# Attention in batches of four key tiles, with row-tiled scores, maxima in turn and split GpSimd additions

## The chip, the cores and the metric

The kernel runs on one core of one Trainium2 chip. The metric is the time of one execution in microseconds of the device (us). Engines are named as in the profile: PE (TensorE's matmuls), PEld (its weight loads), DVE (VectorE), ACT (ScalarE), POOL (GpSimd), and SP (SyncE, whose queue, SPq, issues the DMAs).

## The reference

Two layers work on a sequence of 2048 tokens of width 1024. Each layer projects the normalized input to attention heads, a short convolution and a 2-D Fourier mixer, multiplies each with a gate, joins them and projects back. The change touches the attention: 8 query heads of width 64, which share 2 key/value heads. In float32 it is

```python
scores = jnp.einsum('bqkgd,bskd->bkgqs', qb, k) * HEAD_DIM ** -0.5
p = jax.nn.softmax(scores, axis=-1)
o = jnp.einsum('bkgqs,bskd->bqkgd', p, v)        # every query sees all 2048 keys
y_attn = o * jax.nn.silu(g_a)
```

## The kernel before

A layer runs the input projection (`in_proj`), then the attention with the Fourier mixer as background work (`attention`), then the output projection (`out_proj`). The attention has 16 units in a layer: 4 chunks of 512 queries by 4 pairs of heads. A unit handles its two heads together, against 16 key tiles of 128 keys.

Scores are computed with the keys on the partitions: a tile of probabilities is 128 keys by 512 queries for each of two heads. So that the exp can't overflow, the maximum of each query's scores over all keys is found beforehand by a cheaper product with the queries on the partitions (`row_max`): for one of 4 query tiles and one of 4 key chunks, two matmuls of 64 rows, one per head (the head on partitions 0 to 63 and the one on 64 to 127), then a DVE maximum each. 16 such pairs make a unit. When the last is done, the negated maxima are transposed (`guard_row`) and written by two small DMAs over a row of the unit's second query tile, where they act as one more term of the product. They run ahead of the scores: `LEAD` is 6 pairs beyond one unit.

Products keep float32's accuracy by splitting operands into a rounded part (hi) and a rest (lo). The key tile `kk1` holds the hi part twice (rows 0 to 63 and 64 to 127); the query tile of a head, `qq1`, holds its hi part on 64 rows and its lo part on the others, so that one matmul over 128 rows gives two terms. A second matmul pairs `kk2` (a row of ones, then the keys' lo part) with `qq2` (the guard row, then the queries' hi part). `scores` issues these two (lines 854, 855) for each head of a key tile, and ACT takes the exp out of PSUM (line 856) into a probability tile, one of 8 buffers (4 `XA`, 4 `WL`).

`weigh` multiplies the tile with the values (line 866; the two heads write two halves of the partitions of one PSUM bank, so they run on two halves of the array's columns) and adds it to a running sum for the softmax denominator (lines 874, 876): on DVE for the key tiles in `DVE_KT`, on GpSimd for the others. In the last unit of a layer DVE adds all. `sums` turns the running sums into row sums, `finish` multiplies the result by the gate, the reciprocal of the sums and splits it into hi and lo, in steps spread over the batches of the next unit.

`attention` writes the order of PE, ACT, DVE and GpSimd out by hand. It goes through a unit in 6 batches of 3, 3, 2, 3, 3 and 2 key tiles. A batch issues a step of background work (`background`: the Fourier mixer, 28 steps in a layer, 16 of them with matmuls, later the first output weights), the scores of its key tiles, as many pairs of `row_max`, and the weighing of the batch before:

```python
            for kt in tiles:
                self.scores(u, kt)
            self.max_pairs(pairs)
            ...
                for kt in self.BATCHES[c]:
                    self.weigh(self.units[v], kt)
```

PSUM has 8 banks: 7 with the tag `A` (scores, maxima, transposes, sums, Fourier), one with the tag `C` (the weighed sum).

The projections are products over 128 rows; the last part of `in_proj` runs the first maxima (`first_unit`) between its matmuls.

Of the kernel before, what the change touches and what calls it, by code (L numbers as in the profile page):

```python
# [13 lines left out]
P = 128  # L14
D = 1024
S = 2048
# [22 lines left out]
class Trunk:  # L39
# [34 lines left out]
    def setup(self):  # L74
# [10 lines left out]
        self.zero = self.const("zero", [P, 4])  # L85
        nc.gpsimd.memset(self.zero, 0.0)
# [316 lines left out]
    def do_q(self, l, grp, tabs):  # L403
# [5 lines left out]
        def q_trans(ch, sl, qn):  # L409
# [167 lines left out]
    def fourier_mix_mats(self, l):  # L577
# [3 lines left out]
        for b in range(2):  # L581
            fm = self.small("fm", [P, HD], bufs=2)
# [177 lines left out]
    LEAD = 6  # L760
    BATCHES = ((0, 1, 2), (3, 4, 5), (6, 7), (8, 9, 10), (11, 12, 13), (14, 15))
    NBT = len(BATCHES)

    def q_load(self, u):

        src = self.q1[u["ch"]][u["pr"] // 2][:, u["pr"] % 2]
        u["qq1"] = [self.t("TAB", [P, CH], F32R) for _ in range(2)]
        for h in range(2):
            self.nc.sync.dma_start(u["qq1"][h].bitcast(F32), src[:, h, :])
        u["qq2"], u["mx"] = [], [self.small("mx", [P, 4, 4]) for _ in range(2)]  # L770
        u["nm"] = self.small("nm", [P, 2, 4], F32R, bufs=3)

    def q_copy(self, u, h):

        src = self.q1[u["ch"]][u["pr"] // 2][:, u["pr"] % 2, h, :]
        q2 = self.t("QS", [P, CH], F32R)
        for r in ([slice(0, P)] if h else [slice(0, HD), slice(HD, P)]):
            dr = r if h else slice(HD - r.start, P - r.start)
            self.nc.sync.dma_start(q2.bitcast(F32)[dr], src[r])
        u["qq2"].append(q2)  # L780

    def row_max(self, u, i):

        nc = self.nc
        s, kc = i // 4, i % 4
        pss = [self.p("A") for _ in range(2)]
        for h in range(2):
            r = slice(h * HD, (h + 1) * HD)
            nc.tensor.matmul(pss[h], u["qq1"][h][r, s * P:(s + 1) * P], self.kk1[u["kv"]][kc][r], start=True, stop=True)  # L789

        def reduce():
            for h in range(2):
                nc.vector.tensor_reduce(out=u["mx"][h][:, s, kc:kc + 1], in_=pss[h], axis=AX.X, op=ALU.max)  # L793
            if i == 15:
                for h in range(2):
                    nc.vector.tensor_reduce(out=u["nm"][:, h, :], in_=u["mx"][h], axis=AX.X, op=ALU.max, negate=True)
                self.gq.append(u)
        return reduce

    def guard_row(self, u):  # L800
# [6 lines left out]
        for h in range(2):  # L807
            nc.sync.dma_start(u["qq2"][h].bitcast(F32)[0:1, :], nt.bitcast(F32)[4 * h:4 * h + 4, :])

    def max_before(self, i):  # L810

        for ui, u in enumerate(self.units):
# [3 lines left out]
            elif o in (8, 10):  # L816
                self.q_copy(u, o // 2 - 4)

    def max_pairs(self, pairs):

        while self.gq:
            self.guard_row(self.gq.pop(0))
        todo = [self.row_max(self.units[j // 16], j % 16) for j in pairs if 0 <= j < 16 * len(self.units)]
        for reduce in todo:
            reduce()
# [17 lines left out]
    DVE_KT = (0, 3, 8, 11), range(NKT)  # L843

    def scores(self, u, kt):
# [5 lines left out]
        ks = slice((kt % 4) * P, (kt % 4 + 1) * P)  # L851
        for h in range(2):
            ps = self.p("A")
            nc.tensor.matmul(ps, self.kk1[kv][kt // 4][:, ks], u["qq1"][h], start=True, stop=False)  # L854
            nc.tensor.matmul(ps, self.kk2[kv][kt // 4][:, ks], u["qq2"][h], start=False, stop=True)  # L855
            nc.scalar.activation(pt[:, h, :], ps, AF.Exp, scale=HD ** -0.5)  # L856

    def weigh(self, u, kt):
# [8 lines left out]
        w = "d" if kt in self.DVE_KT[u is self.units[-1]] else "p"  # L867
        eng = nc.vector if w == "d" else nc.gpsimd
        acc, pend = u["acc"], u["pend"]
        if acc[w] is None:  # L870
            pend[w].append(pt)
            if len(pend[w]) == 2:
                acc[w] = self.t("WH", [P, 2, CH])
                eng.tensor_tensor(acc[w], pend[w][0], pend[w][1], ALU.add)  # L874
        else:
            eng.tensor_tensor(acc[w], acc[w], pt, ALU.add)  # L876
# [17 lines left out]
    def finish(self, u, k):  # L894
# [5 lines left out]
        elif k == 3:  # L900
# [4 lines left out]
            for h in range(2):  # L905
                nc.sync.dma_start(u["sm"][h * HD:(h + 1) * HD, :], d[h * CH:(h + 1) * CH].partition_broadcast(HD))
        elif k == 4:
            nc.vector.tensor_tensor(u["y"], u["y"], u["sm"], ALU.mult)
        elif k == 5:
# [5 lines left out]
    def attention(self, l):  # L915
        self.yat = {}
        n = len(self.units)
        for g in range((n + 1) * self.NBT):
            ui, b = divmod(g, self.NBT)
            u = self.units[ui] if ui < n else None  # L920
            tiles = self.BATCHES[b]
# [244 lines left out]
```

## Time and profile before

| | |
|---|---|
| time, median of 3 runs | 2721.76 us (2720.47 to 2722.68) |
| the profiled execution: its time, its span | 2718.48 us, 2716.6 us |
| PE busy | 2664.5 us, 98% of the span |
| DVE busy | 1821.2 us, 67% |
| GpSimd busy | 1032.7 us, 38% |
| ACT busy | 891.0 us, 33% |
| mean DMA rate | 102 GB/s |
| maxima, line 793, DVE | 632.9 us in 1024 instructions |
| weighing, line 866, PE | 271.3 and 267.8 us for the two kinds of tile |

The span runs from the first to the last instruction; the time is the execution's own. Busy time of PE says that matmuls were in flight, not that it ran at its peak. The attention of the two layers lies at about 575 to 1193 us and 1906 to 2525 us.

### The profile page before, as it was taken

To read this page: it belongs to the slowest core of one execution; us is meant where nothing else is said; L and a number is where in the kernel's file an instruction comes from. 1 tells how busy PE (TensorE), PEld (TensorE's weight loads), DVE (VectorE), ACT (ScalarE), POOL (GpSimd) and SP (SyncE) were. 2 spreads that over 40 slices of the span, in tenths; PEclk is the share of its full clock that TensorE was granted. 3 is DMA by queue.
4 is the path that set the end of the run, shared out by engine and by line. 5 is a ranking of instruction groups with operands and counts; after the bars stand their busy time and mean duration, and the time that the engine had idled before them with its cause. 6 is when DMAs were issued, how large, how long until landed. Compare 5 with 4: busy or idle time off the path is not lost.

```text
span 2716.6 us, 36918 instructions
## 1 busy us (share of the span) xinstructions
PE 2664.5 (98%) x13748; PEld 1867.2 (69%) x13748; DVE 1821.2 (67%) x3072; ACT 891.0 (33%) x1789; POOL 1032.7 (38%) x597
## 2 busy tenths in 40 slices
PE   7999999999999999999999999999999999999998
PEld 5987898765555555557898889887565555554686
DVE  6655673457788788786785347534678888778655
ACT  3321421133444444430232124211444444444200
POOL 0200020035786777703331001100558777774134
PEclk9999999999999999999999999999999999999999
DMA  9754362333221111144446123522323111111332
GB/s 302 225 138 149 108 189 72 98 101 121 80 58 44 48 48 48 36 129 156 147 132 186 55 94 98 151 79 85 111 74 105 48 48 47 45 31 51 121 132 93
DMA packets 192516, 277.34 MB, mean 102 GB/s; under 512 B 40400, under 2 KB 103248, under 8 KB 191824
## 3 DMA queue, kind: packets, MB, share of 16 engines
q1 hardware_dynamic: 192336, 274.98, 33.1%
q8 instruction: 108, 1.77, 0.3%
q14 instruction: 72, 0.59, 0.1%
HBM read 213.68 MB, written 69.48 MB: 104 GB/s over the span
## 4 chain that ended last, share of the span: by engine, by line
PE 91%; DVE 4%; DMA 2%; issue 1%; POOL 1%; ACT 1%; SPq 0%; POOLq 0%; DVEq 0%; ACTq 0%
PE psC L866 16%; PE psA L854 9%; PE psA L329 8%; PE psA L330 8%; PE psA L331 8%; PE psA L855 8%; PE psA L789 6%; PE psA L1028 4%; PE psA L1026 4%; PE psA L1027 4%; PE psA L302 3%; PE psA L304 3%; PE psA L303 3%; PE psA L885 1%; PE psA L706 1%
## 5 line engine op out<-in xcount | busy, mean ns | idle before, releaser
L793 DVE TENSOR_REDUCE mx<-psA 128x1 f32<-128x512 f32 x1024 | 632.9, 684 | 238.5 <-PE psA L789 236.3
L876 POOL TENSOR_TENSOR WH<-WH,XA 128x1024 f32<-128x1024 f32 x150 | 362.5, 2417 | 211.1 <-ACT XA L856 208.4
L854 PE MATMUL psA<-TAB,KK 128*128 128x512 f32 x1024 | 421.8, 412 | 0.0
L855 PE MATMUL psA<-QS,KK 128*128 128x512 f32 x1024 | 403.3, 394 | 0.0
L329 PE MATMUL psA<-H,WH 128*128 128x512 f32 x1008 | 397.9, 395 | 0.0
L330 PE MATMUL psA<-H,WH 128*128 128x512 f32 x1008 | 393.4, 390 | 0.0
L331 PE MATMUL psA<-H,WL 128*128 128x512 f32 x1008 | 393.0, 390 | 0.0
L876 POOL TENSOR_TENSOR WH<-WH,WL 128x1024 f32<-128x1024 f32 x150 | 361.4, 2409 | 63.2 <-ACT WL L856 53.8
L856 ACT ACTIVATE XA<-psA 128x512 f32<-128x512 f32 x512 | 281.0, 611 | 307.0 <-PE psA L855 226.3
L856 ACT ACTIVATE WL<-psA 128x512 f32<-128x512 f32 x512 | 281.6, 615 | 161.2 <-PE psA L855 161.0
L854 PEld LDWEIGHTS psA<-TAB,KK 128*128 128x128 f32 x1024 | 192.3, 188 | 155.2 <-issue 87.2
L866 PE MATMUL psC<-XA,V 128*64 128x512 f32 x1024 | 271.3, 608 | 5.8 <-DVE EV L899 5.8
L866 PE MATMUL psC<-WL,V 128*64 128x512 f32 x1024 | 267.8, 601 | 0.0
L128 DVE TENSOR_TENSOR WL<-WR,WH 128x512 fp32r<-128x512 f32 (+2 forms) x272 | 126.0, 500 | 210.0 <-ACT WH L125 204.5
L874 POOL TENSOR_TENSOR WH<-WL,XA 128x1024 f32<-128x1024 f32 x30 | 71.0, 2366 | 446.1 <-DVE mx L793 378.4
L329 PEld LDWEIGHTS psA<-H,WH 128*128 128x128 f32 x1008 | 189.6, 188 | 46.3 <-issue 7.4
L302 PE MATMUL psA<-WH,H 128*128 128x256 f32 x768 | 219.8, 287 | 0.0
L125 ACT ACTIVATE WH<-WR 128x512 fp32r<-128x512 f32 (+2 forms) x280 | 119.4, 479 | 305.3 <-PE psA L330 112.1
L855 PEld LDWEIGHTS psA<-QS,KK 128*128 128x128 f32 x1024 | 192.2, 188 | 37.7
L304 PE MATMUL psA<-WH,H 128*128 128x256 f32 x768 | 216.4, 284 | 0.6 <-DVE H L128 0.6
L303 PE MATMUL psA<-WL,H 128*128 128x256 f32 x768 | 216.8, 283 | 0.0
L331 PEld LDWEIGHTS psA<-H,WL 128*128 128x128 f32 x1008 | 189.3, 188 | 39.8
(215 smaller groups left out, 4010.5 us busy)
## 6 DMA issues: line engine op xcount, KB each, us to landing
WR<-in_w_in SPq DMA_DIRECT2D x176, 256.0 KB
WR<-in_w_ada SPq DMA_DIRECT2D x64, 256.0 KB
q<-EV SPq DMA_DIRECT2D x128, 128.0 KB
TAB<-q SPq DMA_DIRECT2D x64, 256.0 KB
H<-dft SPq DMA_DIRECT2D x64, 256.0 KB
XA<-in_x SPq DMA_DIRECT2D x24, 512.0 KB
XA<-x SPq DMA_DIRECT2D x20, 512.0 KB
dft<-in_k_dft SPq DMA_DIRECT2D x32, 256.0 KB
```

Of the source, the lines that this page charges most:

```text
L302: nc.tensor.matmul(ps[:, s2, :], hh[b][:, sl], w1, start=(b == 0), stop=False)
L303: nc.tensor.matmul(ps[:, s2, :], hh[b][:, sl], w2, start=False, stop=False)
L304: nc.tensor.matmul(ps[:, s2, :], hl[b][:, sl], w1, start=False, stop=(b == NB - 1))
L329: nc.tensor.matmul(ps, w1, hh[b], start=(b == 0), stop=False)
L330: nc.tensor.matmul(ps, w1, hl[b], start=False, stop=False)
L331: nc.tensor.matmul(ps, w2, hh[b], start=False, stop=(b == NB - 1))
L793: nc.vector.tensor_reduce(out=u["mx"][h][:, s, kc:kc + 1], in_=pss[h], axis=AX.X, op=ALU.max)
L854: nc.tensor.matmul(ps, self.kk1[kv][kt // 4][:, ks], u["qq1"][h], start=True, stop=False)
L855: nc.tensor.matmul(ps, self.kk2[kv][kt // 4][:, ks], u["qq2"][h], start=False, stop=True)
L856: nc.scalar.activation(pt[:, h, :], ps, AF.Exp, scale=HD ** -0.5)
L866: nc.tensor.matmul(u["pv"][h * HD:(h + 1) * HD, :], v, pt[:, h, :], start=(kt == 0), stop=(kt == NKT - 1))
L876: eng.tensor_tensor(acc[w], acc[w], pt, ALU.add)
```

## The change

- Scores are row-tiled: query tiles now hold both heads (head 0 on rows 0 to 63, head 1 on 64 to 127), one tile for hi and one for lo, and a key tile's scores are four terms, each a pair of 64-row matmuls for the two heads into two PSUM banks. The fourth term takes the guard row: a constant `sel` with ones in rows 0 and 64 picks rows 0 and 64 of a tile `g`, which is loaded with queries first (`guard_load`), and whose two rows the guard's DMAs overwrite.
- A unit is 4 batches of 4 key tiles. In a batch scores (S) and maxima (M) are issued in the order SSMSMSMM, and each pair's DVE maxima right behind its matmuls. `LEAD` is 8.
- The guard transpose is issued at the beginning of the second batch after the last maxima, ahead of background work and scores (`guard_rows`).
- GpSimd's addition of a probability tile is two instructions, one per head, issued in `scores`; DVE's stays one and in `weigh`. DVE takes key tiles 3, 7, 11 and 15.
- The steps of `finish` are spread over 4 batches and the first of the unit after.
- The queries' and keys' layouts follow: `q_trans` stores hi and lo with two DMAs, `do_kv` puts the keys' rest on both halves. The buffer `fm` of `fourier_mix_mats` has one copy.

```diff
+        sel = self.t("HS", [P, P])
+        nc.gpsimd.memset(sel, 0.0)
+        for h in range(2):
+            nc.gpsimd.memset(sel[h * HD:h * HD + 1, :], 1.0)
+        self.sel = self.const("sel", [P, P], F32R)
+        nc.vector.tensor_copy(self.sel, sel)
...
-            for h in range(2):
-                r, o = slice(h * HD, (h + 1) * HD), slice((1 - h) * HD, (2 - h) * HD)
-                nc.sync.dma_start(self.q1[ch][grp][r, :, h, sl], hi.bitcast(F32)[r])
-                nc.sync.dma_start(self.q1[ch][grp][o, :, h, sl], lo.bitcast(F32)[r])
+            for j, t in enumerate((hi, lo)):
+                nc.sync.dma_start(self.q1[ch][grp][:, :, j, sl], t.bitcast(F32))
...
-            nc.vector.tensor_tensor(kl[:, :, :, HD:], k4, khf[:, :, :, 0:HD], ALU.subtract)
-            kl3 = kl.rearrange("p a b d -> p (a b) d")
-            nc.vector.tensor_copy(kl3[:, :, 0:1], self.ones[:, 0:4].unsqueeze(2))
-            nc.vector.tensor_copy(kl3[:, :, 1:HD], self.zero.unsqueeze(2).to_broadcast([P, 4, HD - 1]))
+            for j in range(2):
+                nc.vector.tensor_tensor(kl[:, :, :, j * HD:(j + 1) * HD], k4, khf[:, :, :, 0:HD], ALU.subtract)
...
-            fm = self.small("fm", [P, HD], bufs=2)
+            fm = self.small("fm", [P, HD], bufs=1)
...
-    LEAD = 6
-    BATCHES = ((0, 1, 2), (3, 4, 5), (6, 7), (8, 9, 10), (11, 12, 13), (14, 15))
-    NBT = len(BATCHES)
+    LEAD = 8
+    ORDER = "SSMSMSMM"
+    BATCH = len(ORDER) // 2
+    NBT = NKT // BATCH
...
+        u["q"] = [self.t("TAB", [P, CH], F32R) for _ in range(2)]
+        for j in range(2):
+            self.nc.sync.dma_start(u["q"][j].bitcast(F32), src[:, j, :])
...
-    def q_copy(self, u, h):
...
+    def guard_load(self, u):
+
+        u["g"] = self.t("QS", [P, CH], F32R)
+        self.nc.sync.dma_start(u["g"].bitcast(F32), self.q1[u["ch"]][u["pr"] // 2][:, u["pr"] % 2, 0, :])
...
-            self.gq.append(u)
+            self.gq.append([u, 2])
...
+    def guard_rows(self):
+
+        for e in list(self.gq):
+            e[1] -= 1
+            if not e[1]:
+                self.guard_row(e[0])
+                self.gq.remove(e)
...
-    DVE_KT = (0, 3, 8, 11), range(NKT)
+    DVE_KT = (3, 7, 11, 15), range(NKT)
...
+        k1, k2, (q1, q2) = self.kk1[kv][kt // 4][:, ks], self.kk2[kv][kt // 4][:, ks], u["q"]
+        pss = [self.p("A") for _ in range(2)]
+        terms = (k1, q1), (k1, q2), (k2, q1), (self.sel, u["g"])
+        for i, (k, q) in enumerate(terms):
+            for h in range(2):
+                r = slice(h * HD, (h + 1) * HD)
+                nc.tensor.matmul(pss[h], k[r], q[r], start=i == 0, stop=i == len(terms) - 1)
         for h in range(2):
-            ps = self.p("A")
-            nc.tensor.matmul(ps, self.kk1[kv][kt // 4][:, ks], u["qq1"][h], start=True, stop=False)
-            nc.tensor.matmul(ps, self.kk2[kv][kt // 4][:, ks], u["qq2"][h], start=False, stop=True)
-            nc.scalar.activation(pt[:, h, :], ps, AF.Exp, scale=HD ** -0.5)
+            nc.scalar.activation(pt[:, h, :], pss[h], AF.Exp, scale=HD ** -0.5)
+        self.add(u, kt, pt, "p")
...
+        if w == "d":
+            self.nc.vector.tensor_tensor(acc[w], a, pt, ALU.add)
         else:
-            eng.tensor_tensor(acc[w], acc[w], pt, ALU.add)
+            for h in range(2):
+                self.nc.gpsimd.tensor_tensor(acc[w][:, h], a[:, h], pt[:, h], ALU.add)
...
+        for g in range((n + 2) * self.NBT):
...
+            if 0 < ui <= n and b == 2:
+                self.sums(self.units[ui - 1])
+            self.guard_rows()
...
+            self.background()
+            at = {"S": 0, "M": 0}
+            for c in self.ORDER:
+                if c == "M":
+                    self.max_pairs((pair + at[c],))
+                elif u:
+                    self.scores(u, first + at[c])
+                at[c] += 1
             if 0 < g <= n * self.NBT:
                 v, c = divmod(g - 1, self.NBT)
+                for j in range(self.BATCH):
+                    self.weigh(self.units[v], self.BATCH * c + j)
...
+            for back in (1, 2):
+                if 0 <= ui - back < n:
+                    self.finish(self.units[ui - back], b + self.NBT * (back - 1))
```

## Rows read from the trace of the kernel before

**Rows 1.** The page's first part: busy time, share of the span, instructions.

```profile
PE 2664.5 (98%) x13748; PEld 1867.2 (69%) x13748; DVE 1821.2 (67%) x3072; ACT 891.0 (33%) x1789; POOL 1032.7 (38%) x597
```

**Rows 2.** Chain of waits from 900 to 980 us: start, length, what.

```profile
904.54 2.74 PE psC L866 x12
...
917.70 1.87 PE psC L866 x8
...
941.65 2.73 PE psC L866 x12
```

**Rows 3.** Windows, one unit: length, busy of each engine, clock, DMA share, GB/s.

```profile
904.54:941.65 37.11, 37.11 (x180) 19.16 (x181) 29.82 (x43) 17.21 (x34) 26.36 (x12) 1.00 0.17 44
```

**Rows 4.** PE in order of time: start, length, line, matmuls merged.

```profile
903.57 0.98 PE L789 MATMUL psA<-KK,TAB 64*128 64x512 f32 x6
...
909.97 0.40 PE L855 MATMUL psA<-QS,KK 128*128 128x512 f32 x1
910.30 0.74 PE L789 MATMUL psA<-KK,TAB 64*128 64x512 f32 x4
910.96 1.08 PE L866 MATMUL psC<-WL,V 128*64 128x512 f32 x4
...
913.69 0.50 PE L854 MATMUL psA<-TAB,KK 128*128 128x512 f32 x1
914.03 0.40 PE L855 MATMUL psA<-QS,KK 128*128 128x512 f32 x1
```

**Rows 5.** Line 789 over the whole span: least, median and most ns.

```profile
L789 PEld LDWEIGHTS psA<-KK,TAB x1024: 182/183/187, 517.5 to 2471.6; 64*128 64x128 f32 x171
L789 PE MATMUL psA<-KK,TAB x1024: 384/395/502, 517.5 to 2471.8; 64*128 64x512 f32 x171
```

**Rows 6.** PE in order of time around a guard transpose.

```profile
922.36 0.22 PE L804 MATMUL psA<-identr,nm 128*8 128x128 f32 x1
922.51 1.41 PE L789 MATMUL psA<-KK,TAB 64*128 64x512 f32 x6
```

**Rows 7.** PE in order of time, a Fourier step (L708) ahead of scores.

```profile
631.48 0.39 PE L708 MATMUL psA<-H,H 128*128 128x512 f32 x1
631.71 0.39 PE L854 MATMUL psA<-TAB,KK 128*128 128x512 f32 x1
631.94 0.39 PE L855 MATMUL psA<-QS,KK 128*128 128x512 f32 x1
```

**Rows 8.** Line 876 on DVE over the whole span.

```profile
L876 DVE TENSOR_TENSOR WH<-WH,WL x44: 1210/3108/3394, 613.1 to 2523.6; 128x1024 f32<-128x1024 f32 x44
```

**Rows 9.** GpSimd and DVE in order of time: additions, Fourier multiplications (L737).

```profile
736.00 1.29 POOL L737 TENSOR_TENSOR H<-H,H 128x512 f32<-128x512 f32 x1
...
742.02 2.26 POOL L737 TENSOR_TENSOR H<-H,H 128x512 f32<-128x512 f32 x1
...
903.65 2.37 POOL L876 TENSOR_TENSOR WH<-WH,XA 128x1024 f32<-128x1024 f32 x1 [2.52 <-ACT XA L856]
906.10 2.36 POOL L876 TENSOR_TENSOR WH<-WH,WL 128x1024 f32<-128x1024 f32 x1
...
931.53 3.27 DVE L876 TENSOR_TENSOR WH<-WH,WL 128x1024 f32<-128x1024 f32 x1
```

**Rows 10.** DVE and ACT in order of time: maxima, exps.

```profile
904.11 3.68 DVE L793 TENSOR_REDUCE mx<-psA 128x1 f32<-128x512 f32 x6 [1.44 <-PE psA L789]
...
914.53 1.09 ACT L856 ACTIVATE XA<-psA 128x512 f32<-128x512 f32 x2 [3.41 <-PE psA L855]
```

**Rows 11.** SP's queue in order of time: reciprocal out, back in, guard row.

```profile
921.28 0.32 SPq L903 DMA_DIRECT2D rc<-rc  x1
922.69 1.10 SPq L906 DMA_DIRECT2D HS<-rc  x2
923.90 1.29 SPq L808 DMA_DIRECT2D QS<-HS  x2
```

**Rows 12.** PE in order of time, end of the first layer's attention.

```profile
1163.47 1.08 PE L866 MATMUL psC<-XA,V 128*64 128x512 f32 x4 [2.89 <-DVE EV L899]
...
1193.03 0.64 PE L885 MATMUL psA<-WH,ones 128*32 128x256 f32 x8 [2.42 <-DVE WH L876]
```

More of the change, by code (lines that the diff above doesn't have):

```diff
@@ L788, in row_max @@
             r = slice(h * HD, (h + 1) * HD)
-            nc.tensor.matmul(pss[h], u["qq1"][h][r, s * P:(s + 1) * P], self.kk1[u["kv"]][kc][r], start=True, stop=True)
-        def reduce():
+            nc.tensor.matmul(pss[h], u["q"][0][r, s * P:(s + 1) * P], self.kk1[u["kv"]][kc][r], start=True, stop=True)
+        for h in range(2):
+            nc.vector.tensor_reduce(out=u["mx"][h][:, s, kc:kc + 1], in_=pss[h], axis=AX.X, op=ALU.max)
+        if i == 15:
             for h in range(2):
[L793 to L796, printed above, removed]
-                self.gq.append(u)
-        return reduce
+                nc.vector.tensor_reduce(out=u["nm"][:, h, :], in_=u["mx"][h], axis=AX.X, op=ALU.max, negate=True)
+            self.gq.append([u, 2])
     def guard_row(self, u):
@@ L815, in max_before @@
                 self.q_load(u)
-            elif o in (8, 10):
-                self.q_copy(u, o // 2 - 4)
+            elif o == 8:
+                self.guard_load(u)
     def max_pairs(self, pairs):
[L821 to L825, printed above, removed]
+        for j in pairs:
+            if 0 <= j < 16 * len(self.units):
+                self.row_max(self.units[j // 16], j % 16)
     def first_unit(self, l):
@@ L866, in weigh, with add @@
             nc.tensor.matmul(u["pv"][h * HD:(h + 1) * HD, :], v, pt[:, h, :], start=(kt == 0), stop=(kt == NKT - 1))
[L867 to L868 removed]
+        self.add(u, kt, pt, "d")
+    def add(self, u, kt, pt, w):
+        if (kt in self.DVE_KT[u is self.units[-1]]) != (w == "d"):
+            return
         acc, pend = u["acc"], u["pend"]
[L870 removed]
+        a = acc[w]
+        if a is None:
             pend[w].append(pt)
[L872 to L876 removed]
+            if len(pend[w]) < 2:
+                return
+            acc[w] = self.t("WH", [P, 2, CH])
+            a = pend[w][0]
+        if w == "d":
+            self.nc.vector.tensor_tensor(acc[w], a, pt, ALU.add)
+        else:
+            for h in range(2):
+                self.nc.gpsimd.tensor_tensor(acc[w][:, h], a[:, h], pt[:, h], ALU.add)
     def sums(self, u):
@@ L917, in attention @@
         n = len(self.units)
-        for g in range((n + 1) * self.NBT):
+        for g in range((n + 2) * self.NBT):
             ui, b = divmod(g, self.NBT)
             u = self.units[ui] if ui < n else None
-            tiles = self.BATCHES[b]
-            pairs = [NKT * (ui + 1) + self.LEAD + kt for kt in tiles]
-            for j in pairs:
-                self.max_before(j)
-            if ui and b == 2:
+            first = self.BATCH * b
+            pair = NKT * (ui + 1) + self.LEAD + first
+            for j in range(self.BATCH):
+                self.max_before(pair + j)
+            if 0 < ui <= n and b == 2:
                 self.sums(self.units[ui - 1])
+            self.guard_rows()
             if ui == n - 1 and b == 0:
@@ L930, in attention @@
             self.background()
-            if u:
-                for kt in tiles:
-                    self.scores(u, kt)
-            self.max_pairs(pairs)
+            at = {"S": 0, "M": 0}
[5 more added lines that the diff above has]
+                at[c] += 1
             if 0 < g <= n * self.NBT:
                 v, c = divmod(g - 1, self.NBT)
-                for kt in self.BATCHES[c]:
-                    self.weigh(self.units[v], kt)
-            if u and b == 4:
+                for j in range(self.BATCH):
+                    self.weigh(self.units[v], self.BATCH * c + j)
+            if u and b == 2:
                 u["ga"] = self.t("EV", [P, CH])
                 self.nc.sync.dma_start(u["ga"], self.ga[u["pr"]][u["ch"]])
-            if ui:
-                self.finish(self.units[ui - 1], b)
+            for back in (1, 2):
+                if 0 <= ui - back < n:
+                    self.finish(self.units[ui - back], b + self.NBT * (back - 1))
     def wout_consts(self, l):
```

21 lines of the change are left out of this document (5 added, 16 removed).

## The prediction

> **What bounds the kernel now.** I read the profile from the whole to one batch: the page, the chain, the windows, the instructions in order of time. On the page the reader sees PE busy 98% of the span and no other engine near it [rows 1]: what PE doesn't save, nothing saves. The profiled execution took 2718.48 us beside a span of 2716.6; the sum is made against it. The median of the runs, 2721.76, lies 3.3 us above, and I carry that over.
>
> The change lives in the attention. There the chain of waits goes from PE to PE, and the same point returns 37.11 us later, one unit (two heads, 512 queries, 16 key tiles) [rows 2]. Within it PE has no hole, DVE works 29.82 us and GpSimd 26.36 [rows 3]. So a unit is the sum of PE's starts, and in those one sees what a batch costs beyond its work. Each batch has three stretches: scores S on the full array, maxima M on two halves of its rows, weighing W on two halves of its columns. Within a stretch a full matmul of 512 columns starts some 0.235 us after the one before (0.23 to 0.24 in [rows 7]). At each border it is longer:
> - S to M: 909.97 to 910.30, 0.33, so +0.09 [rows 4]. In M a pair of matmuls takes as long as one full one: six take 0.98 and four 0.74, the third pair costs 0.24 [rows 4]. Less the 0.395 of one [rows 5], the second pair starts 0.345 after the first, so +0.105. This border costs 0.195.
> - M to W: the second pair stands at 910.645, W at 910.96: 0.315, so +0.08.
> - W itself: three tiles take 2.74 on the chain and two 1.87 [rows 2], so 0.87 a tile and 0.13 more for entering and leaving.
> - The first score after W lasts 913.69 to 914.03, 0.34 [rows 4]: +0.105.
>
> So a batch pays 0.195 for S to M and 0.08 + 0.13 + 0.105 = 0.315 for going through W and back.
>
> **The change part by part.**
>
> *Row-tiled scores.* A head's tile was two matmuls over 128 rows; now both heads' tiles are four pairs of 64-row matmuls: four full starts become four pairs. No row shows a row-tiled pair that accumulates. From below the price of a pair is a full start, 0.235; from above two starts in a row, 0.47. I take 0.235, the row that is nearest: M's pairs have the same 64 rows, 512 columns and two PSUM banks, and cost 0.24 [rows 4]. S itself then neither gains nor loses.
>
> S and M now share one layout, and the border between them goes. In a layer maxima run beside scores in 88 of the 96 batches (14 units of 6, and 4 batches of the fifteenth; the maxima are 22 pairs ahead): 88 x 0.195 = 17.2 us.
>
> *Batches of four.* 16 units of 6 batches become 16 of 4, 32 trips through W fewer: 32 x 0.315 = 10.1 us a layer.
>
> *What this adds on PE.* The guard transpose (full array) stood between S and M, where a border was due anyway. Now it stands between W and row-tiled scores: 0.15 to the next start [rows 6], against the 0.06 or so that it added before: 0.09 x 15 = 1.4 us. The Fourier steps in the background also stand ahead of S. They are full-array and flow into full-array scores without a step, 631.48 to 631.71 [rows 7]; now a border is due: 16 steps with matmuls x 0.195 = 3.1 us. The prologue in the input projection gets one step of maxima more, two borders, 0.4 us.
>
> A layer: 17.2 + 10.1 - 1.4 - 3.1 - 0.4 = 22.4; two layers 44.8 us.
>
> *Maxima in turn (SSMSMSMM): do the seven PSUM banks hold?* Counted from the start of a batch, the last pair of the first tile starts at 0.34 + 2 x 0.235 = 0.81; exps follow a last start by 0.5 (914.03 to 914.53) and take 1.09 a tile [rows 4, 10]: tile 1 to 2.4, tile 2 to 3.5, tile 3 to 4.6. The first maxima stand at 1.98, and DVE takes them from 2.5, 0.61 each (3.68 for six) [rows 10]: to 3.1 and 3.75. The fourth tile wants two banks at 3.4. The first maximum's has come free, the second tile's is just about to: a stall of 0.1 to 0.35 us a batch, 0.4 to 1.4 a unit. Today's order stalls too: six maxima take 1.41 behind the transpose instead of 0.98 [rows 4, 6], 0.43 a unit. I take the two as equal and keep both ends: 29 units (those with maxima) x 0.43 = 12 us better, 29 x 1.0 = 29 us worse.
>
> *GpSimd's additions.* A 128x1024 addition takes 2.37 us, and 2.45 from start to start; a 128x512 instruction took 1.29 [rows 9]. 11 additions a unit become 22: 22 x (1.29 + 0.08) = 30.1 us. From below, half of 2.37 gives 27.8. DVE and GpSimd keep each other out: a DVE addition takes 1.21 at least and 3.27 beside GpSimd's [rows 8, 9], and a 512-wide GpSimd multiplication took 2.26 beside a DVE addition [rows 9]. Five such DVE instructions a unit: three additions cost GpSimd up to 0.97 each, two shorter ones perhaps 0.6: 30.1 + 4.1 = 34.2. A unit of 37.11 - 1.7 = 35.4 still covers that, by a hair. If the cover goes, exps wait for probability tiles. The other side: DVE now waits for at most 1.29 instead of 2.37, some 2 us of DVE a unit and nothing in time, as PE covers DVE with 7 us to spare.
>
> Moving the additions into the score step changes neither their order nor what they need (the exp). Four new tiles and the four of the batch before fill the eight buffers, so GpSimd may be about a batch late before an exp waits.
>
> *The guard row.* A batch of four is 4 x (4 x 0.235 + 0.24 + 0.87) + 0.3 = 8.5 us. The guard transpose now opens the unit's last batch, and the fourth term of the next unit's first tile needs the row 8.5 + 0.8 = 9.3 us later. Its two DMAs stand in SP's queue behind the reciprocal's: 2.62 from that write, 921.28, to the guard row's issue [rows 11]. DVE makes the reciprocal up to 1.3 us into the batch (behind the maxima and an addition of the batch before); then 2.6 to the issue, 1.3 for both, 1.4 to land (a small write at 921.28 frees the next at 922.69 [rows 11]): 6.6. It is 2.7 us early.
>
> *The rest.* Four query stores of 128 KB become two of 256 KB; a unit loads three query tiles of 256 KB instead of four; on the key side one subtraction and two copies become two subtractions. All lies beside a PE that doesn't wait in those stages: zero. The second buffer of the mixing weights goes, so a small load waits for two products: 0 to 1.4 us a layer (the landing above), taken as zero.
>
> *The end of a layer's attention.* PE stands 2.89 us before W and 2.42 before the sums, both waiting for DVE [rows 12]. The last unit's additions are all DVE's. Its last batch now has four, 4 x 1.21 = 4.8 us, against 3.5 us of W, so a wait of 1.3 to 3 stays before the sums; the other may go. Taken as no change; ends 5 us better and 3 worse a layer.
>
> Sum: 2721.8 - 44.8 = 2677 us.
>
> One rule speaks against the row tiles. M's loads take 0.183 us and still its pairs follow at 0.24 [rows 4, 5], so the load of the next weights for the same rows runs under the matmul. The Trainium skill (TensorE: Matmul & The Clock Gate, Part 3, The mechanism) says that a weight load overlaps running matmuls only where its row group is another one. By the rule the load would be added to every pair; by the rows, to none.
>
> **The rivals.**
> 1. *The pairs don't keep pace* (ends slower). A load that isn't hidden adds 0.183 to each pair: 2 layers x 256 tiles x 4 pairs = 2048 x 0.183 = 375 us, so 3052; two starts in a row instead of a pair, 0.235 more, give 3158. It decides from 44.8 / 2048 = 0.022 us a pair. For it: M has at most three pairs on end and never accumulates. Against it: M's third pair at 0.24.
> 2. *The guard row comes late* (even or slower). If something else stands ahead in SP's queue by more than 2.7 us, each unit's first tile waits for the rest. It decides from 44.8 / 30 = 1.5 us a unit, so at 4.2 us of delay; 4 to 5 give 2716 to 2746. Against it: the queue is nearly empty there [rows 11].
> 3. *GpSimd becomes the bound.* With 1.2 for each of five meetings it needs 36.1 a unit, 0.7 over PE's: 29 x 0.7 = 20, so 2697: still faster. For it: the hair above.
> 4. *PSUM stalls* at their upper end: 2706.
> 5. *The change gives more*: stalls gone (12) and both waits at the end gone (10): 2655.
>
> **How the numbers follow.** Forecast as summed 0.64 (2664 to 2692 by the small bounds), rival 3 0.12, rival 4 0.08, rival 5 0.06, rivals 2 and 1 0.05 each. The range 2655 to 2703 leaves out rivals 1 and 2 and the edges of 4 and 5. Measurement tells 0.2% (5.4 us) from no change. Faster takes the forecast and rivals 3 to 5, less a little for those that add up: 0.88. Rival 1 and most of rival 2 are slower, 0.09; same 0.03.
>
> **What would show it.** Score matmuls in pairs of nearly one start, the next pair 0.235 later; 0.235 instead of 0.33 between S and M; four W stretches of 3.6 us a unit; a unit of 35.4 us; GpSimd's additions near 1.3 us, 30 to 34 us a unit. Wrong would be: pairs over 0.26 apart, PE idle before the last score term of a unit's first tile, or exps that wait for GpSimd.

## The result and the profile after

| | before | after |
|---|---|---|
| median (4 runs each) | 2722.22 us (2720.47 to 2722.72) | 2677.19 us (2676.53 to 2679.53) |
| ratio, 95% interval | | 0.9837 [0.982, 0.9854] |
| profiled execution: time, span | 2718.48, 2716.6 us | 2679.53, 2677.5 us |

The forecast was 2677. The two profiled executions lie 39.1 us apart, the medians 45.0: the one shown of before was a quick one, the one of after the slowest of its four.

The page of the changed kernel, its busy times:

```profile
PE 2623.0 (98%) x15796; PEld 1877.8 (70%) x15796; DVE 1777.1 (66%) x3057; ACT 909.7 (34%) x1789; POOL 1130.3 (42%) x929
```

PE is still the bound [rows 1]. GpSimd has 332 instructions more and works 98 us longer; nothing of that is seen in the time. One unit in the windows (columns as in [rows 3]):

```profile
897.64:933.04 35.40, 35.40 (x243) 19.36 (x241) 28.73 (x43) 17.87 (x34) 29.40 (x23) 1.00 0.13 38
```

A unit is 35.40 us, 35.4 was forecast. PE has no hole in it, DVE works 28.73 us, GpSimd 29.40. One batch of it from its second tile on, PE in order of time (start, length, line):

```profile
899.45 0.85 PE L860 MATMUL psA<-TAB,KK 64*128 64x512 f32 x6
900.14 0.39 PE L860 MATMUL psA<-QS,sel 64*128 64x512 f32 x2
900.36 0.40 PE L786 MATMUL psA<-KK,TAB 64*128 64x512 f32 x2
900.60 0.85 PE L860 MATMUL psA<-TAB,KK 64*128 64x512 f32 x6
901.29 0.39 PE L860 MATMUL psA<-QS,sel 64*128 64x512 f32 x2
901.52 0.39 PE L786 MATMUL psA<-KK,TAB 64*128 64x512 f32 x2
901.83 0.97 PE L860 MATMUL psA<-TAB,KK 64*128 64x512 f32 x6
902.64 0.39 PE L860 MATMUL psA<-QS,sel 64*128 64x512 f32 x2
902.87 0.63 PE L786 MATMUL psA<-KK,TAB 64*128 64x512 f32 x4
903.42 1.08 PE L873 MATMUL psC<-XA,V 128*64 128x512 f32 x4
```

- A tile's three pairs and the pair with `sel` go by at 0.23 each: 899.45 to 900.14 is 0.69 for three.
- Scores to maxima take 0.22 (900.14 to 900.36) and back 0.24: no border, where [rows 4] have 0.33.
- The fourth tile starts 0.31 after the maxima instead of 0.23, and its first pair lasts 0.105 longer (0.81 to the `sel` pair instead of 0.69). It waits for two banks: 0.18 in this batch. The unit's other batches pay 0.18, 0.10 and 0.16.
- W still costs its entry (902.87 to 903.42 is 0.55 for two pairs, so 0.32 for the second) and its exit.

Line 786 over the whole span (least, median, most ns) and the way from a Fourier step into scores:

```profile
L786 PEld LDWEIGHTS psA<-KK,TAB x1024: 182/184/186, 523.0 to 2427.3; 64*128 64x128 f32 x171
...
626.05 0.39 PE L708 MATMUL psA<-H,H 128*128 128x512 f32 x1
626.37 0.97 PE L860 MATMUL psA<-TAB,KK 64*128 64x512 f32 x6
627.18 0.39 PE L860 MATMUL psA<-QS,sel 64*128 64x512 f32 x2
```

A load is still 0.184 us long and costs nothing beside a pair [rows 5]. From Fourier to scores it is 0.32 and 0.81 instead of the flowing 0.23 of [rows 7]: the 0.2 of a border.

The guard row: PE's transpose, then SP's queue, in order of time:

```profile
916.60 0.22 PE L799 MATMUL psA<-identr,nm 128*8 128x128 f32 x1
916.75 0.50 PE L860 MATMUL psA<-TAB,KK 64*128 64x512 f32 x2
...
917.50 0.32 SPq L919 DMA_DIRECT2D rc<-rc  x1
918.90 1.15 SPq L922 DMA_DIRECT2D HS<-rc  x2
920.14 1.30 SPq L803 DMA_DIRECT2D QS<-HS  x2
```

0.15 behind the transpose as in [rows 6]; the same order in the queue as in [rows 11], the row's DMAs issued by 921.44, 3.8 us before the next unit's first tile (925.28) and 4.65 before that tile's `sel` pair (926.09). The additions, DVE's by line 889 and GpSimd's groups (busy us, mean ns):

```profile
L889 DVE TENSOR_TENSOR WH<-WH,WL x74: 1209/1753/2339, 610.1 to 2483.1; 128x1024 f32<-128x1024 f32 x74
...
L892 POOL TENSOR_TENSOR WH<-WH,XA 128x512 f32<-128x512 f32 x420 | 598.3, 1446 | 156.4 <-ACT XA L862 156.4
L892 POOL TENSOR_TENSOR WH<-WH,WL 128x512 f32<-128x512 f32 x180 | 227.9, 1287 | 0.0
```

DVE's 120 additions took 2.30 us on average before, 62 of them over 2.4 us (the group in [rows 8] has a median of 3.1); now it is 1.73, and the longest takes 2.34. GpSimd's take 1.29, as its multiplications did [rows 9], except where they meet a DVE addition: some two a unit take 2.3, hence the 1446 ns. Last, PE's holes at the mixing weights and the ends of the attentions:

```profile
500.57 0.63 PE L591 MATMUL psA<-fm,HS 128*128 128x64 f32 x4 [2.59 <-DMA fm<-in_f_mix]
...
1172.71 0.64 PE L901 MATMUL psA<-WH,ones 128*32 128x256 f32 x8 [2.02 <-DVE WH L889]
...
2484.34 0.64 PE L901 MATMUL psA<-WH,ones 128*32 128x256 f32 x8 [2.38 <-DVE WH L889]
```

The wait ahead of W is gone, the one ahead of the sums stays [rows 12], and a new one, 2.59 us here and 2.37 in the second layer, stands at the mixing weights.

**Where the time came from.** From the first maxima (517.47 before, 522.99 after) to the last sums (1193.03 and 1172.71) the first layer's attention became 25.84 us shorter; the second, counted in the same way, 24.46. Of that, 2.89 and 2.92 are the wait ahead of W, 0.40 and 0.05 the shorter one ahead of the sums. 22.55 and 21.5 are left for the terms of the sum, which had 22.4. Outside the attentions the profiled execution of after takes 11.2 us longer: 5.0 at the mixing weights; the other 6.2 are in small pieces and about what sets these two executions off from their medians.

### The profile page after: what moved, and what is told of

The parts are those of the page before. It is cut to its first block, busy times and chain, and to the rows that moved or that the text cites. A ratio compares the mean times of both kernels' runs of the same rounds, so it can differ in the third digit from the quotient of the medians.

```text
span 2677.5 us, 41599 instructions
## 1 busy us (share of the span) xinstructions
PE 2623.0 (98%) x15796; PEld 1877.8 (70%) x15796; DVE 1777.1 (66%) x3057; ACT 909.7 (34%) x1789; POOL 1130.3 (42%) x929
## 4 chain that ended last, share of the span: by engine, by line
PE 92%; DVE 3%; DMA 3%; ACT 1%; issue 1%; POOL 1%; SPq 0%; POOLq 0%; DVEq 0%; ACTq 0%
PE psA L860 19%; PE psC L873 16%; PE psA L333 9%; PE psA L334 8%; PE psA L335 8%; PE psA L786 5%; PE psA L1049 4%; PE psA L1047 4%; PE psA L1048 4%; PE psA L306 3%; PE psA L308 3%; PE psA L307 3%; PE psA L901 1%; DMA WR<-in_w_in 1%; PE psA L706 1%
## 5 line engine op out<-in xcount | busy, mean ns | idle before, releaser
L892 POOL TENSOR_TENSOR WH<-WH,XA 128x512 f32<-128x512 f32 x420 | 598.3, 1446 | 156.4 <-ACT XA L862 156.4
L860 PE MATMUL psA<-TAB,KK 64*128 64x512 f32 x3072 | 469.4, 407 | 0.8 <-ACT XA L862 0.7
L860 PEld LDWEIGHTS psA<-TAB,KK 64*128 64x128 f32 x3072 | 273.6, 184 | 136.8 <-issue 51.9
L892 POOL TENSOR_TENSOR WH<-XA,WL 128x512 f32<-128x512 f32 x60 | 76.0, 1288 | 430.0 <-ACT WL L862 238.0
L892 POOL TENSOR_TENSOR WH<-WH,WL 128x512 f32<-128x512 f32 x180 | 227.9, 1287 | 0.0
L333 PEld LDWEIGHTS psA<-H,WH 128*128 128x128 f32 x1008 | 189.9, 188 | 46.8 <-issue 8.1
L335 PEld LDWEIGHTS psA<-H,WL 128*128 128x128 f32 x1008 | 189.7, 188 | 40.4
L334 PEld LDWEIGHTS psA<-H,WH 128*128 128x128 f32 x1008 | 189.8, 188 | 37.7
L860 PE MATMUL psA<-QS,sel 64*128 64x512 f32 x1024 | 205.5, 389 | 0.0
```

The source lines that it names most:

```text
L333: nc.tensor.matmul(ps, w1, hh[b], start=(b == 0), stop=False)
L334: nc.tensor.matmul(ps, w1, hl[b], start=False, stop=False)
L335: nc.tensor.matmul(ps, w2, hh[b], start=False, stop=(b == NB - 1))
L860: nc.tensor.matmul(pss[h], k[r], q[r], start=i == 0, stop=i == len(terms) - 1)
L892: self.nc.gpsimd.tensor_tensor(acc[w][:, h], a[:, h], pt[:, h], ALU.add)
```

## The experiments

Twelve kernels. "Unit" is the time from one unit's sums to the next in steady state. Each ratio is to runs of the kernel before on the same chip, whose medians were 2719 to 2722 us; differences below are taken to those. The diffs show the lines that matter; the rest of an edit follows from them.

| kernel | median us | ratio to before, 95% | unit us |
|---|---|---|---|
| before | 2722 | 1 | 37.2 |
| after | 2677.19 | 0.9837 [0.982, 0.9854] | 35.4 |
| e4 heads apart | 2676.27 | one run | 35.4 |
| e12 full-array scores, in turn | 2754.15 | 1.0118 [1.0101, 1.0135] | 38.7 |
| e2 full-array, blocks | 2834.64 | 1.0428 [1.041, 1.0445] | 39.5 to 43.7 |
| e6 row tiles, blocks | 2787.5 | 1.0258 [1.0243, 1.0274] | 39.4 |
| e1 row tiles, 3-3-2, blocks | 2774.47 | 1.0206 [1.019, 1.0221] | 38.1 |
| e5 row tiles, 3-3-2, in turn | 2714.89 | 0.9989 [0.9979, 0.9998] | 36.2 |
| e8 maxima first, two `fm` | 2698.89 | 0.9929 [0.9912, 0.9945] | 35.9, one of 37.1 |
| e7 whole GpSimd additions | 2684.08 | 0.9874 [0.9859, 0.9888] | 35.4 |
| e9 14 tiles on GpSimd | 2699.73 | 0.9922 [0.9907, 0.9937] | 35.4 |
| e10 guard row a batch later | 2816.28 | 1.0344 [1.0323, 1.0365] | 40.9 |
| e3 two `fm` | 2673.08 | 0.9829 [0.9814, 0.9844] | 35.4 |
| e11 last unit shared, two `fm` | 2683.88 | 0.9856 [0.9839, 0.9872] | 35.4 |

### Row tiles alone and not

**e12**: the kernel before, and so its scores, with the changed kernel's batches, order and additions (`LEAD` stays 6).

```diff
-    BATCHES = ((0, 1, 2), (3, 4, 5), (6, 7), (8, 9, 10), (11, 12, 13), (14, 15))
+    ORDER = "SSMSMSMM"
+    BATCHES = tuple(tuple(range(4 * b, 4 * b + 4)) for b in range(4))
...
+            for h in range(2):
+                self.nc.gpsimd.tensor_tensor(acc[w][:, h], a[:, h], pt[:, h], ALU.add)
```

> The changed kernel with the scores of before: two full-array matmuls per head instead of four pairs of 64-row ones; batches of 4, SSMSMSMM, GpSimd's additions split and issued in the score step as in the changed kernel. A head's tile is then complete after its own two matmuls, so banks come free as early as before; what it pays is the border between full array and row halves, three times a batch into maxima (0.195 each in the kernel before) and two times back into scores (0.1 to 0.195 each, no row). That is 0.78 to 0.98 a batch more than the changed kernel, 3.1 to 3.9 a unit: units of 38.5 to 39.3 and 2768 to 2790 us. If the borders within the row-halved stretch cost less than this (short stretches may hide them), units of 36 to 37 and about 2700 to 2725; if a batch of four can't be fed by seven banks without row tiles either, about 2834, the time of the block order with full-array scores.

PE in order of time around one pair of maxima:

```profile
908.16 0.40 PE L864 MATMUL psA<-QS,KK 128*128 128x512 f32 x1
908.49 0.50 PE L790 MATMUL psA<-KK,TAB 64*128 64x512 f32 x2
908.92 0.50 PE L863 MATMUL psA<-TAB,KK 128*128 128x512 f32 x1
909.26 0.39 PE L864 MATMUL psA<-QS,KK 128*128 128x512 f32 x1
```

From 908.16 to 909.26 three starts take 1.10 instead of 0.70: a pair of maxima between full-array scores costs 0.39 in borders. PE has no hole in the attention until its end, so the banks hold. Units are 38.65 us, as the borders said, 3.25 over the changed kernel. The time is 14 us under the range, which was reckoned with the full difference in every unit: the first three of a layer, with the Fourier steps, differ by 2.5, and this kernel has two `fm`. Row tiling is thus worth 77 us in this order, and the borders account for it: two pairs between scores and one entry into the last pairs are 0.39 + 0.39 + 0.195 a batch, 3.9 a unit, less the 0.6 that the changed kernel waits for banks: 3.3.

**e4**: the order of the pairs in the program.

```diff
-        for i, (k, q) in enumerate(terms):
-            for h in range(2):
+        for h in range(2):
+            for i, (k, q) in enumerate(terms):
```

> The changed kernel with the four score terms of one head first, then the four of the other, so that neighbours on PE share their rows and can't be a pair. If a pair of row tiles takes the time of one start because the two run at once, and a load for the same rows still hides under a matmul, a tile takes 8 starts of 0.235 instead of 4: 512 x 0.94 = 481 us more, 3158. If a load for the rows in use can't be hidden, each start is 0.235 + 0.183: 3.34 a tile instead of 0.94, 1230 more, 3907. If pairs weren't what makes it fast, 2677.

Neither. Two tiles of scores on PE, in order of time:

```profile
898.18 0.97 PE L860 MATMUL psA<-TAB,KK 64*128 64x512 f32 x6
898.87 0.51 PE L860 MATMUL psA<-QS,sel 64*128 64x512 f32 x2
899.11 0.50 PE L786 MATMUL psA<-KK,TAB 64*128 64x512 f32 x2
```

A tile still takes 0.93 (898.18 to 899.11), and the time is the changed kernel's, though of a single run. One by one the starts are 898.182, .298, .412, .527, .640, .763 for the six, .872 and .995 for the two with `sel`. In the program the first `sel` is fourth; in the trace it stands behind all six others. So the second head's terms start between the first head's, 0.115 behind them: each half of the rows goes through its own matmuls, one every 0.23 with the next load under it. That PE and not the compiler put them so can be told from the semaphore updates in the trace: in most tiles of e4 both heads' `sel` matmuls raise PE's semaphore by several at once, as the last of four of their own would, while in the changed kernel one of the two raises it by one. A pair need not stand side by side in the program.

The Trainium skill (TensorE: Matmul & The Clock Gate, Part 3, The mechanism) says that a load overlaps only matmuls of another row group and that matmuls start in program order. This run contradicts both: each half's loads of 0.184 fit into starts 0.23 apart, and the second head's starts lie between the first's. Rival 1 rested on the first.

### Batches, blocks and turns

**e2** and **e6**: batches of four as blocks, S four times, then M four times, once in the kernel before and once in the changed one.

```diff
-    BATCHES = ((0, 1, 2), (3, 4, 5), (6, 7), (8, 9, 10), (11, 12, 13), (14, 15))
+    BATCHES = tuple(tuple(range(4 * b, 4 * b + 4)) for b in range(4))
```
```diff
-    ORDER = "SSMSMSMM"
+    ORDER = "SSSSMMMM"
```

> The kernel before with 4 batches of 4 key tiles, four scores and then four maxima, full-array scores, one GpSimd addition per tile. By the count of trips through the weighing alone: 2722 - 20 = 2702. By the bank count it is slower: after four score tiles the third pair of maxima waits for an exp until about 5.15 us into the batch instead of 4.45, the fourth for another until 5.7, about 1.0 us a batch x 116 batches = 116, so about 2818. I expect the second; 2702 would say that seven banks are enough without taking turns.

> The changed kernel with four scores and then four maxima in a batch (SSSSMMMM). Nothing changes on PE but the order. If the banks are what the turns are for, the third and fourth pair of maxima wait for exps: at least the 1.7 us a batch by which the second experiment's units were longer than its borders allow, 29 units x 4 x 1.7 = 197 us, near 2875. If turns are a matter of DVE's evenness alone and PE doesn't wait, 2677.

**e1** and **e5**: row tiles and split additions with the batches of before, as blocks and in turn.

```diff
-    ORDER = "SSMSMSMM"
+    BATCHES = ((0, 1, 2), (3, 4, 5), (6, 7), (8, 9, 10), (11, 12, 13), (14, 15))
```
```diff
+            for c in {3: "SSMSMM", 2: "SMSM"}[len(tiles)]:
```

> The changed kernel with the old batches of 3, 3, 2, 3, 3, 2 key tiles, scores of a batch first and then its maxima: row-tiled scores alone (and the split GpSimd additions). By my sum the borders between scores and maxima are worth 2 x 17.2 us, the transposes and Fourier steps ahead of row-tiled scores and the longer prologue cost 2 x 4.9, and the wait for the small mixing weight that the changed kernel's trace shows costs 5: 2722 - 34 + 10 + 5 = 2703. The rival, that the bigger batches bring most of it, expects 2712 or more.

> As the first experiment (row-tiled scores in batches of 3, 3, 2), with scores and maxima in turn (SSMSMM for three tiles, SMSM for two). The first one was slower than the kernel before: its maxima wait for exps in every batch, since a row-tiled tile's first head is complete only with its second and its two banks come free later. If that bank wait was all that went wrong, taking turns gives the 2703 that I had worked out, a unit of 36.0 us. If row-tiled scores cost something else in small batches, it stays near 2774 (a unit of 38.1).

**e8**: the maxima first.

```diff
-    ORDER = "SSMSMSMM"
+    ORDER = "MSMSMSMS"
...
-            fm = self.small("fm", [P, HD], bufs=1)
+            fm = self.small(("fm", "gk")[b], [P, HD], bufs=1)
```

> The changed kernel with the order MSMSMSMS and the second mixing weight in a buffer of its own. By the bank count with maxima first, no score or maximum has to wait within a batch, where the fourth score tile of SSMSMSMM waits 0.07 and then pays 0.105 for a start without preloaded weights: 0.17 x 116 batches = 20 us at most if every batch has it, 5 if every fourth. With the 4 of the third experiment: 2652 to 2669. If the border W to maxima or the later exps of the last tile cost more, 2673 or above.

A stretch of PE (and of ACT in e1), in order of time, first of e1, then e2, e6 and e8:

```profile
898.66 0.96 PE L859 MATMUL psA<-TAB,KK 64*128 64x512 f32 x6
899.95 1.09 ACT L861 ACTIVATE XA<-psA 128x512 f32<-128x512 f32 x2 [3.19 <-PE psA L859]
...
901.53 1.52 PE L785 MATMUL psA<-KK,TAB 64*128 64x512 f32 x6
```
```profile
919.19 0.99 PE L789 MATMUL psA<-KK,TAB 64*128 64x512 f32 x2 [0.55 <-ACT WL L856]
921.86 0.54 PE L789 MATMUL psA<-KK,TAB 64*128 64x512 f32 x1 [1.68 <-DVE mx L793]
922.33 1.97 PE L866 MATMUL psC<-XA,V 128*64 128x512 f32 x4
```
```profile
914.45 2.00 PE L786 MATMUL psA<-KK,TAB 64*128 64x512 f32 x8
```
```profile
834.01 0.96 PE L860 MATMUL psA<-TAB,KK 64*128 64x512 f32 x5 [1.13 <-DVE mx L789]
```

Six maxima in a block take 1.52 in e1 where PE alone needs 0.86, eight take 2.00 in e6 instead of 1.09; they wait for banks, which in e1 exps free, in e6 exps and maxima. The time that e1 and e6 miss is this: row tiles fill two banks at once and complete both heads only with the last pair, so exps begin later than with a full-array tile, whose first head is done after two matmuls. The first exp of a batch follows the first score by 1.29 us in e1 (898.66 to 899.95) and by 0.84 in the kernel before (913.69 to 914.53 [rows 4, 10]). In e1 that took all of the border's gain and more (unit 38.1, before 37.2; one unit of 45.1 adds 7 us). In turn, the same batches take 36.2 (e5), of the 36.0 expected; its 2715 still misses 2703 by one unit a layer behind the Fourier steps (40.4 and 39.3) and the 0.2 of the others. The hand count of 1.0 us a batch behind e2's expectation fits e6 too (39.4 less 35.4, by four), whose own expectation, 1.7 a batch and 2875, missed by 87 us. In e2 the count isn't all: behind such holes the granted clock falls to its lower level (0.57 from 923 to 926 us, and the first four products of W take 1.97 instead of 1.08). Over the attentions it is 0.96 and 0.97 where the kernel before has 1.00; by these means, as an estimate, some 40 of e2's 115 us are the clock. e8, at 2699, missed its 2652 to 2669, and the mistake was mine: behind maxima that come first PE waits for banks that DVE, busy with the batch before, frees late.

So the parts don't add up. Against before: row tiles in turn -4 us (e5), batches of four as blocks +115 (e2) or in turn +32 (e12), row tiles in batches of four as blocks +68 (e6) and in turn -45.

### GpSimd

**e7** undoes the split, **e9** gives GpSimd two tiles more.

```diff
-            for h in range(2):
-                self.nc.gpsimd.tensor_tensor(acc[w][:, h], a[:, h], pt[:, h], ALU.add)
+            self.nc.gpsimd.tensor_tensor(acc[w], a, pt, ALU.add)
```
```diff
-    DVE_KT = (3, 7, 11, 15), range(NKT)
+    DVE_KT = (7, 15), range(NKT)
```

> The changed kernel with GpSimd's addition as one instruction for both heads. My theory: nothing in time (2672 to 2682), for PE covers DVE and GpSimd; in the trace DVE's additions take up to 3.3 us again and GpSimd's busy time falls by some 4 us a unit. The rival, that the halves are what lets DVE keep up, expects 10 us or more above the changed kernel.

> GpSimd takes 14 of a unit's 16 tiles instead of 12: 26 instructions instead of 22. In the changed kernel 22 instructions kept it busy for 30.1 us of a 35.4 us unit, 1.37 each. If that is its price, 26 need 35.6 us, over the unit: GpSimd becomes the bound, exps wait for probability tiles, and units are 35.6 to 36.5 long (more where Fourier multiplications stand between), so 2685 to 2740 us. If GpSimd has more room than its busy time shows, because half of what lengthens its instructions is DVE's additions, of which one stays instead of three, the time stays within 2674 to 2682 us.

A unit of e7 in the windows, and DVE's additions in it (least, median, most ns over the span):

```profile
902.00:937.40 35.40, 35.40 (x243) 19.45 (x241) 28.32 (x43) 17.86 (x35) 27.97 (x12) 1.00 0.13 39
...
L889 DVE TENSOR_TENSOR WH<-WH,WL x74: 1211/1224/2943, 607.1 to 2486.7; 128x1024 f32<-128x1024 f32 x74
```

e7 lies between its two cases: steady units don't change; the 7 us are in the units behind the Fourier steps (36.2 and 36.1) and in the holes ahead of the sums (4.85 instead of 2.02 in the first layer). GpSimd's busy time falls by 1.5 us a unit, not by 4. DVE's additions reach 3.4 us again, but only five of the 120 take over 2.4; their mean is 1.49 us, less than the changed kernel's 1.73. So it isn't the split that made DVE's additions shorter than before: with e7's whole additions they are shorter still, and what remains is the rest of the change (the order, the tiles, additions issued with the scores), which no run takes apart. The split shortens the longest of these waits.

e9's time is in the range, but mostly for another reason. Two units of e9 in the windows:

```profile
753.80:797.30 43.50, 38.08 (x243) 20.75 (x245) 32.70 (x42) 17.85 (x34) 32.20 (x27) 0.92 0.13 36
...
879.20:914.60 35.40, 35.40 (x243) 19.64 (x245) 27.11 (x41) 17.85 (x34) 33.56 (x27) 1.00 0.13 39
```

The steady unit holds 26 instructions in 33.56 us and stays 35.40: GpSimd is not the bound. What breaks are the units around its Fourier multiplications, three in the first layer (753.80 to 879.20): GpSimd is busy for 106.3 us in them, as much as PE needs for three, and they take 125.4. In the changed kernel too GpSimd is at its limit beside these multiplications, busy for 70.67 of 70.84 us in two units (777.46 to 848.30), but there PE doesn't wait. DVE, GpSimd and PE in one of them, in order of time:

```profile
779.45 9.91 DVE L924 TENSOR_TENSOR EV<-EV,HS 128x512 f32<-128x512 f32 x1
...
786.32 2.49 POOL L892 TENSOR_TENSOR WH<-WH,XA 128x512 f32<-128x512 f32 x2
796.39 2.53 POOL L892 TENSOR_TENSOR WH<-WH,WL 128x512 f32<-128x512 f32 x2 [7.58 <-ACT WL L862]
...
790.01 1.64 PE L860 MATMUL psA<-TAB,KK 64*128 64x512 f32 x5 [5.42 <-DVE mx L789]
```

A DVE multiplication that takes 0.68 elsewhere takes 9.91 beside an unbroken row of GpSimd instructions, and ends only 0.6 us after GpSimd has run out of work (788.81). Behind it stand DVE's maxima, which hold the banks, for which PE waits 5.42 us; and GpSimd ran dry because no exp came. Such holes make up most of e9's loss.

The Trainium skill (SBUF — State Buffer, SBUF: two separate sides) says that whichever of the two starts first has the shared port pair for the whole instruction and the other waits until then. If the pair changed hands at the end of an instruction, DVE's wait would end with one of GpSimd's, 1.29; here it lasted through seven.

### The guard row

```diff
-            self.gq.append([u, 2])
+            self.gq.append([u, 3])
```

> The guard transpose opens a unit's first batch instead of the last batch of the unit before; all else as in the changed kernel. The prediction reckoned 6.6 us from there until the row has landed and 2.7 us to spare; a batch is 8.5 us, so now the row is some 5.8 us late at most, less where DVE and the queue are free: the transpose, its copy, 1.3 us for two DMAs and 1.4 to land are about 3.5 us from the transpose on, against 1.1 us until the first tile's fourth term. PE then waits 2.4 to 5.8 us in each of 30 units: 72 to 174 us, so 2749 to 2851 us. If the row's way is hidden by something else, or the other terms fill it, the time stays at 2677.

PE in order of time at the first tile of a unit, and windows over the same stretch (the seventh number is the granted clock):

```profile
918.38 0.96 PE L860 MATMUL psA<-TAB,KK 64*128 64x512 f32 x6
922.60 0.49 PE L860 MATMUL psA<-QS,sel 64*128 64x512 f32 x1 [3.25 <-DMA QS<-HS]
923.29 0.79 PE L860 MATMUL psA<-QS,sel 64*128 64x512 f32 x1 [0.20 <-DMA QS<-HS]
...
922.60:924.70 2.10, 1.90 (x7) 1.35 (x9) 0.00 (x0) 1.18 (x2) 0.00 (x0) 0.62 0.50 126
924.70:926.70 2.00, 2.00 (x12) 1.57 (x10) 0.84 (x2) 1.10 (x3) 0.56 (x1) 0.54 0.00 0
926.70:928.87 2.17, 2.17 (x20) 1.62 (x16) 1.91 (x4) 1.64 (x4) 2.17 (x3) 1.00 0.00 0
```

The wait is there and has the size expected, 3.3 us. A steady unit grew by 5.5, though. The second head's row comes 0.7 later (923.29), as its DMA is the second of the two. And after the hole the granted clock is 0.62 and 0.54, the lower of its two levels (1.2 GHz) for most of 4 us: six pairs follow at 0.42 instead of 0.23, 1.2 us more. The rest is the start behind the wait. So a hole of 3.3 us on PE is paid 1.7 times. In each layer eight units grew by 5.5 us, the two behind the Fourier steps by some 10, the first three by 1.2 and the last by 2 to 4: 70 us a layer, and the 139 us are in the expected range. Rival 2 was real, and a batch away.

### What was left at the borders of the stages

**e3** gives `fm` a second buffer (the `fm` line of e8's diff alone). **e11** adds GpSimd to the last unit.

```diff
-    DVE_KT = (3, 7, 11, 15), range(NKT)
+    DVE_KT = (3, 7, 11, 15), range(1, NKT, 2)
```

> The changed kernel with the second mixing weight in a buffer of its own (one that is free at that time). The changed kernel's trace has PE idle for 2.59 and 2.37 us ahead of the mixing products, which the trace of before doesn't have. If that wait is on the path, 2677 - 5 = 2672. If something behind it takes the time back, 2677.

> Two buffers for the Fourier mixer's small weights, and in a layer's last unit GpSimd adds the even tiles and DVE the odd ones instead of DVE all. If the gap ahead of the last sums (2.0 and 2.4 us) is DVE's four additions at the end, two stay, done before the weighing, and the gap falls to some 0.5 us: about 3 us under the 2673 of two buffers alone, so 2670. If it is the time from the last weighing product or from GpSimd's additions on, the gap stays or grows, and the time is 2673 or more.

e3: the holes at the mixing weights are gone, and the median is 4.1 us lower; the intervals overlap, so only the holes are shown. In its profile another stands in a later unit, DVE and PE in order of time:

```profile
2146.48 7.69 DVE L889 TENSOR_TENSOR WH<-WL,WL 128x1024 f32<-128x1024 f32 x1
...
2154.48 1.60 PE L860 MATMUL psA<-TAB,KK 64*128 64x512 f32 x5 [3.97 <-DVE HS L801]
```

That is e9's mechanism, here with an addition of 1.21 us held for 7.69 while GpSimd ran from 2141.91 to 2153.09 with no pause. Behind it stood the copy of the guard's transpose.

e11 was slower than e3 by 11 us, the second of its two cases. DVE and PE at the end of the first layer's attention:

```profile
1168.14 2.54 DVE L889 TENSOR_TENSOR WH<-WH,WL 128x1024 f32<-128x1024 f32 x2
...
1170.74 1.08 PE L901 MATMUL psA<-WH,ones 128*32 128x256 f32 x8 [4.50 <-DVE WH L889]
```

GpSimd was done at 1164, and DVE still had two additions to make behind the splitting of output weights, which had run at half its speed beside GpSimd. The hole grew from 2.0 to 4.5, and from 2.4 to 4.5 in the second layer. That explains 5 us; e11's profile has a hole like e3's too, which doesn't set the two apart. Why the medians differ by 11 isn't settled.

## Why the prediction was right

- **Borders** (17.2 a layer) and **W trips** (10.1): held. 0.22 instead of 0.33 between scores and maxima, four W stretches a unit, 35.40 a unit. e12 shows the border from the other side, 3.25 us a unit.
- **Pairs at 0.235**: 0.23. The nearest row, M's third pair, was the right one. Rival 1 is out, and e4 shows that it is out even where pairs aren't neighbours.
- **Fourier border** (3.1): 0.2 a step, as forecast. **Guard transpose** (1.4): 0.15 to the next start, as forecast.
- **PSUM stalls taken as equal**: 0.10 to 0.18 a batch, within the 0.1 to 0.35, 0.6 in the unit shown against the 0.43 of before. But the argument was incomplete: it counted banks, and the row tiles' later exps with them, for one order only, and did not see that in blocks this delay costs more than the borders give. e1 is where that would have gone wrong: the sum's own terms, without turns, gave 2703, and it took 2774.
- **GpSimd at 34.2 of 35.4 "by a hair"**: mis-sized in the steady unit. 29.40, and 33.56 with two tiles more. The instruction's 1.29 was right, and so was the 0.97 of a meeting with DVE (2.3 instead of 1.29); but it meets two DVE instructions a unit, not five, and for the others DVE does the waiting. Beside its Fourier multiplications the hair was real: 70.67 of 70.84 us.
- **"DVE waits at most 1.29"**: wrong as a bound (7.69 in e3, 9.91 in e9), right in the changed kernel's own profile, where the longest addition takes 2.34 of which 1.21 is its own. That the split brings DVE time back is not shown: without it DVE's additions are shorter on average (e7).
- **The guard row 2.7 us early**: it was earlier. Its DMAs were issued 4.65 us ahead of the `sel` pair; in e10 each head's `sel` went on 1.1 us behind the end of its issue (922.20 to 923.29), so by this estimate some 3.5 us were left. e10 gives what a miss costs.
- **`fm`** (0 to 1.4 a layer, taken as 0): 2.5. The small load waits for products that use the old weights, then takes its own time; I had only its landing.
- **The end of the attention** (no change): the wait ahead of W went, 2.9 a layer, and the one ahead of the sums stayed. These 5.8 and the 5.0 of `fm` cancelled. That the median meets 2677 to a fraction of a us is therefore luck; the attention's 22.55 and 21.5 a layer against 22.4 are not.

## What to carry to other kernels

Where stretches of a kernel use the array in different shapes, the price is at the borders (0.2 us each here, 0.39 for one small pair in between), and bringing two stretches to one shape pays if no matmul becomes slower. A shape that completes several tiles at once hands its results on later; before adopting it, count the banks again and give the consumers' work turns among the producers', as it is the order that decided for row tiles in batches of four between +2.6% (e6) and -1.6%. And price a hole on PE with the slower stretch behind it, not with its length alone.

## What the runs showed of the hardware

- The two row halves of PE go through their queued matmuls independently: a start that stands fifth in the program came second (e4), at no cost (2676 against 2677 us, one run).
- A hole of 3.3 us on PE was followed by 4 us of which most ran at the lower clock level (0.62 and 0.54 granted); with the second row's 0.7 it cost 5.5 (e10).
- DVE can be held for as long as GpSimd issues 128x512 additions without a pause: 9.91 us for an instruction of 0.68, 7.69 for one of 1.21 (e9, e3). It isn't so each time: in the changed kernel GpSimd is nearly as unbroken in two units (busy for 70.67 of 70.84 us), and no addition of DVE takes over 2.34. What decides it stays open. Splitting GpSimd's instructions shortened the longest of DVE's ordinary additions (3.4 to 2.3), not their mean (1.49 without the split, 1.73 with it; e7).
